# Residual add and RMS norm over 65,536 rows: each tile's store is queued behind five minimum-reductions on VectorE

## Chip, cores, metric

One core of a Trainium2 chip. The metric is device microseconds of one execution. The kernel before takes 3724.74 us (median of 4 runs, 3724.70 to 3724.87). All runs quoted are fast, with a granted clock of 1.0.

## The reference

```python
batch, seq, dim = 32, 2048, 2048          # x, residual: float32; gamma: ones(dim)
z = x + residual
rms = np.sqrt(np.mean(z ** 2, axis=-1, keepdims=True) + eps)
return (z / rms * gamma).astype(np.float32)
```

That is 537 MB of x and 537 MB of residual to read and 537 MB of output to write.

## The kernel before

The rows are cut into tiles of 128 partitions x 7 rows x 2048 columns, 7168 KB each (the first two are smaller, the last is handled in four pieces): 74 tiles, numbered 0 to 73. There are two buffers `z` for x, worked on in place and stored from, and one area `r_area` of 11 rows for the residual. SyncE issues the loads of x and the stores, on one queue; ScalarE issues the residual's loads, on another. VectorE adds, ScalarE takes sums of squares and root, VectorE scales.

```python
z = [sb(f"z{p}", [P, R, D]) for p in range(2)]      # R = 7, D = 2048
r_area = sb("r_area", [P, R + STEP, D])             # STEP = 4
... # cut
def sp_turn(sp, t):                                  # SyncE, tile i - 1 goes out
    i = t.i
    t.wait(sp, "done", -1)
    inc(sp.dma_start(out=rows(o_f, i - 1), in_=z[(i - 1) % 2][:, : sizes[i - 1], :]), "s_out", i - 1)
    ... # cut
    t.wait(sp, "s_out", -1)                          # the store has landed
    load_x(sp, t, 1)                                 # x of tile i + 1, same buffer, same queue
... # cut
def dve_turn(v, t, own):                             # VectorE
    i, p = t.i, t.p
    t.wait(v, "x_in")
    t.wait(v, "r_in")
    (a0, b0), (a1, b1) = parts(i)                    # 3 or 4 of the 7 rows
    inc(add(v, i, a0, b0), "add_a", i)               # lets ScalarE load the next residual
    inc(add(v, i, a1, b1), "add_b", i)
    for h, (a, b) in enumerate(parts(i)):
        n = b - a
        t.wait(v, "rms_a" if h == 0 else "rms_b")
        v.reciprocal(out=rstd[p][h][:, :n], in_=rms[p][h][:, :n]).then_inc(dve, U)
        v.wait_ge(dve, own(i, h))
        ins = scale(v, i, a, b, rstd[p][h])
    inc(ins, "done", i)
```

Of the kernel before, what the change touches and what calls it, by code (L numbers as in the profile page):

```python
# [9 lines left out]
def kernel(  # L10
# [5 lines left out]
    eps: float,  # L16
    out: bass.AP,
):



# [7 lines left out]
    P = nc.NUM_PARTITIONS  # L29
# [20 lines left out]
    last = n_tiles - 1  # L50

    LO = 3
# [12 lines left out]
    def sb(name, shape):  # L65
        return ctx.enter_context(nc.sbuf_tensor(name, shape, fp32))
# [6 lines left out]
    def sem(name):  # L73
        sems.append(ctx.enter_context(nc.semaphore(name)))
        return sems[-1]
# [6 lines left out]
    ssq = [[sb(f"ssq{p}{h}", [P, 4]) for h in range(2)] for p in range(2)]  # L82
    rms = [[sb(f"rms{p}{h}", [P, 4]) for h in range(2)] for p in range(2)]
    rstd = [[sb(f"rstd{p}{h}", [P, 4]) for h in range(2)] for p in range(2)]
    tail_ssq = sb("tail_ssq", [P, R])
    tail_rms = sb("tail_rms", [P, R])
    tail_rstd = sb("tail_rstd", [P, R])
# [8 lines left out]
    dve = sem("dve_own")  # L96
    act = sem("act_own")
    s_tail = sem("s_tail")
    tail_ev = {k: sem(f"tail_{k}") for k in ("add", "rms", "done")}


# [7 lines left out]
    def parts(i):  # L109
        if i == 0:  # L110
            return [(0, 2), (2, sizes[0])]
        k = sizes[i] if i < 2 else R
        return [(STEP, k), (0, STEP)] if i % 2 else [(0, R - STEP), (R - STEP, R)]
# [15 lines left out]
    def inc(ins, kind, i):  # L129
        return ins.then_inc(ev[kind][i % 2], U)  # L130
# [38 lines left out]
    def add(v, i, a, b):  # L169
        e = entry(i)  # L170
        s = z[i % 2][:, a:b, :]
        return v.tensor_add(out=s, in0=s, in1=r_area[:, e + a : e + b, :])  # L172

    def scale(v, i, a, b, rs, c=0):
        for g in range(a, b):
            s = z[i % 2][:, g, :]
            ins = v.scalar_tensor_tensor(  # L177
                out=s,
                in0=s,
                scalar=rs[:, c + g - a : c + g - a + 1],  # L180
                in1=gamma_tile[:, :],
                op0=mult,
                op1=mult,
            )
        return ins

    def dve_turn(v, t, own):
# [3 lines that stand above are left out]
        (a0, b0), (a1, b1) = parts(i)  # L191
        inc(add(v, i, a0, b0), "add_a", i)
# [4 lines that stand above are left out]
            v.reciprocal(out=rstd[p][h][:, :n], in_=rms[p][h][:, :n]).then_inc(dve, U)  # L197
            v.wait_ge(dve, own(i, h))
            ins = scale(v, i, a, b, rstd[p][h])
        inc(ins, "done", i)  # L200


    class Chain:
# [69 lines left out]
    def vector_program(v):  # L273
        v.memset(eps_tile[:, :], float(eps))  # L274
        v.memset(stage, 0.0).then_inc(tail_ev["add"], 1)  # L275
        v.wait_ge(g_in, 4 * U)
        v.stream_shuffle(gamma_tile[:, :].rearrange("p (a b) -> p a b", a=16), stage, [0] * 32)  # L277
        for i in range(LO):
            dve_turn(v, Turn(i), lambda i, h: (2 * i + h + 1) * U)
        with v.Fori(0, 2 * n_iter, 2) as it:  # L280
            for i in range(LO, LO + 2):
                dve_turn(v, Turn(i, it), lambda i, h: it * (2 * U) + (2 * i + h + 1) * U)
        for i in range(HI, last):
            dve_turn(v, Turn(i), lambda i, h: (2 * i + h + 1) * U)
        base = 2 * last * U
        t = Turn(last)
        t.wait(v, "r_in")

        def tail_scale(k):
            a, b = tail[k]  # L290
            v.wait_ge(tail_ev["rms"], k + 1)
            v.reciprocal(out=tail_rstd[:, a:b], in_=tail_rms[:, a:b]).then_inc(dve, U)  # L292
            v.wait_ge(dve, base + (k + 1) * U)
            scale(v, last, a, b, tail_rstd, a).then_inc(tail_ev["done"], 1)

        for k, (a, b) in enumerate(tail):
            v.wait_ge(x_tail[k], U)
            add(v, last, a, b).then_inc(tail_ev["add"], 1)
            if k:
                tail_scale(k - 1)  # L300
        tail_scale(len(tail) - 1)
# [21 lines left out]

    sync_program(nc.sync)
    vector_program(nc.vector)
    scalar_program(nc.scalar)

# [40 lines left out]
```

## Time and profile before

| | before |
|---|---|
| time | 3724.74 us |
| span in the profile | 3723.7 us |
| VectorE, ScalarE, GpSimd busy | 62%, 29%, 0% |
| DMA row | 9 in all 40 slices |

The DMA row gives how busy the 16 DMA engines are. Of the kernel before, with 40 slices of 93 us each:

```profile
GB/s 421 431 434 435 434 434 435 434 435 435 434 434 434 434 434 434 434 434 433 434 434 434 434 434 434 434 434 434 434 434 434 434 434 434 434 434 434 434 432 398
```

What SyncE waits for, in the kernel before (who waited for what: us in total, times, longest):

```profile
SPq L135 <- DMA out_dram<-z: 2828.4, 71, 43.0
SPq L153 <- DVE z L177: 735.1, 73, 32.2
```

About 10 us in each tile it waits for VectorE's done, and about 40 us for the landing of the store that this releases. The second wait is four times the first; the prediction is about what it is made of.

### The profile page before, as it was taken

The numbers are of one execution on the slowest core, as the hardware profiler recorded it, in microseconds if no ns is written. First come the engines' busy times: TensorE is split into PE (matmuls) and PEld (weight loads), VectorE is DVE, ScalarE is ACT, GpSimd is POOL, SyncE is SP. The second block draws the span as 40 slices with busy tenths as digits, with TensorE's granted clock in tenths as the row PEclk, the third lists the DMA queues.
The fourth block names the chain that finished last, engine by engine and source line by source line (L and its number), as shares of the span: only waits on it lengthen the run. The fifth ranks groups of instructions, "written<-read, shape, count | busy, mean of one in ns | idle before, by whom it ended". The sixth has DMA issues, their size and how long they took to land.

```text
span 3723.7 us, 3798 instructions
## 1 busy us (share of the span) xinstructions
DVE 2302.6 (62%) x816; ACT 1072.4 (29%) x1176; POOL 0.2 (0%) x4
## 2 busy tenths in 40 slices
DVE  5666665566665566665566665566665566665566
ACT  2233322233322233322233322233322233322233
POOL 0000000000000000000000000000000000000000
DMA  9999999999999999999999999999999999999999
GB/s 421 431 434 435 434 434 435 434 435 435 434 434 434 434 434 434 434 434 433 434 434 434 434 434 434 434 434 434 434 434 434 434 434 434 434 434 434 434 432 398
DMA packets 32963, 1610.68 MB, mean 433 GB/s; under 512 B 3712, under 2 KB 3776, under 8 KB 3776
## 3 DMA queue, kind: packets, MB, share of 16 engines
q1 hardware_dynamic: 22592, 1082.17, 67.2%
q10 hardware_dynamic: 10368, 528.49, 32.8%
q14 instruction: 3, 0.02, 0.0%
HBM read 1073.77 MB, written 536.87 MB: 433 GB/s over the span
## 4 chain that ended last, share of the span: by engine, by line
DMA 67%; DVE 22%; issue 9%; ACT 2%; SPq 0%; DVEq 0%; ACTq 0%
DMA out_dram<-z 39%; DMA z<-in_x_dram 27%; DVE z L172 15%; DVE z L177 7%; ACT sq_junk L223 1%; ACT rms L231 0%; DVE rstd L197 0%; SPq L259 0%; DVEq L127 0%; DVE r_area L275 0%; ACTq L211 0%; ACTq L127 0%; SPq L141 0%; DVE tail_rstd L292 0%; SPq L162 0%
## 5 line engine op out<-in xcount | busy, mean ns | idle before, releaser
L172 DVE TENSOR_TENSOR z<-z,r_area 128x8192 f32<-128x8192 f32 (+2 forms) x150 | 1109.5, 7437 | 1252.5 <-DMA z<-in_x_dram 1252.5
L223 ACT ACTIVATE sq_junk<-z 128x2048 f32<-128x2048 f32 x512 | 963.4, 1882 | 2617.1 <-DVE z L172 2605.7
L177 DVE SCALAR_TENSOR_TENSOR z<-z,rstd,gamma_tile 128x2048 f32<-128x2048 f32 x505 | 1153.6, 2344 | 5.2
L197 DVE RECIPROCAL rstd<-rms 128x4 f32<-128x4 f32 (+2 forms) x146 | 25.3, 173 | 130.8 <-ACT rms L231 130.8
L223 ACT ACTIVATION_READ_ACCUMULATOR sq_junk<-z 128x1 f32 x512 | 95.5, 186 | 0.0
L231 ACT ACTIVATE rms<-ssq,eps_tile 128x4 f32<-128x4 f32 (+2 forms) x146 | 43.3, 297 | 13.4
L177 DVE SCALAR_TENSOR_TENSOR z<-z,tail_rstd,gamma_tile 128x2048 f32<-128x2048 f32 x7 | 16.2, 2345 | 0.1
L277 DVE LOAD_MASK_SELECT gamma_tile<-r_area x1 | 0.0, 14 | 16.1 <-DMA r_area<-in_gamma_dram 16.1
L277 DVE STREAM_SHUFFLE gamma_tile<-r_area 128x2048 f32<-128x2048 f32 x1 | 2.3, 2290 | 0.0
L275 DVE MEMSET r_area<- 128x2048 f32 x1 | 1.8, 1765 | 0.4 <-issue 0.4
L223 ACT ACT_TABLE_LOAD x1 | 1.3, 1283 | 0.9 <-SPq L77 0.9
L231 ACT ACT_TABLE_LOAD x1 | 1.3, 1283 | 0.1
L231 ACT ACTIVATE tail_rms<-tail_ssq,eps_tile 128x2 f32<-128x2 f32 (+1 forms) x4 | 1.2, 295 | 0.1
L274 DVE MEMSET eps_tile<- 128x1 f32 x1 | 0.1, 59 | 1.0 <-SPq L77 1.0
L292 DVE RECIPROCAL tail_rstd<-tail_rms 128x2 f32<-128x2 f32 (+1 forms) x4 | 0.6, 158 | 0.0
L349 POOL MEMSET const-bfloat16-1.0<- 128x1 bf16 x1 | 0.1, 101 | 0.0
L349 POOL MEMSET const-uint8-127<- 128x1 uint8 x1 | 0.1, 101 | 0.0
L349 POOL MEMSET const-float32-0.0<- 128x1 f32 x1 | 0.1, 98 | 0.2 <-issue 0.2
L349 POOL MEMSET const-float32-1.0<- 128x1 f32 x1 | 0.1, 98 | 0.0
## 6 DMA issues: line engine op xcount, KB each, us to landing
r_area<-in_residual_dram ACTq DMA_DIRECT2D x72, 7168.0 KB, 35.5
z<-in_x_dram SPq DMA_DIRECT2D x71, 7168.0 KB, 27.5
out_dram<-z SPq DMA_DIRECT2D x71, 7168.0 KB, 40.8
z<-in_x_dram SPq DMA_DIRECT2D x3, 2048.0 KB, 17.9
out_dram<-z SPq DMA_DIRECT2D x3, 2048.0 KB, 15.0
r_area<-in_residual_dram SPq DMA_DIRECT2D x1, 5120.0 KB, 25.0
z<-in_x_dram SPq DMA_DIRECT2D x1, 5120.0 KB, 36.7
out_dram<-z SPq DMA_DIRECT2D x1, 5120.0 KB, 26.5
```

The lines of the kernel that those rows point to most:

```text
L172: return v.tensor_add(out=s, in0=s, in1=r_area[:, e + a : e + b, :])
L177: ins = v.scalar_tensor_tensor(out=s, in0=s, scalar=rs[:, c + g - a : c + g - a + 1], in1=gamma_tile[:, :], op0=mult, op1=mult,)
L197: v.reciprocal(out=rstd[p][h][:, :n], in_=rms[p][h][:, :n]).then_inc(dve, U)
L223: s.activation(out=sq_junk[:, :], in_=src[:, g, :], func=Act.Square, accum_out=sq[:, g - a : g - a + 1],)
L231: return s.activation(out=rm, in_=sq[:, : b - a], func=Act.Sqrt, bias=eps_tile[:, :], scale=inv_d)
L274: v.memset(eps_tile[:, :], float(eps))
L275: v.memset(stage, 0.0).then_inc(tail_ev["add"], 1)
L277: v.stream_shuffle(gamma_tile[:, :].rearrange("p (a b) -> p a b", a=16), stage, [0] * 32)
L292: v.reciprocal(out=tail_rstd[:, a:b], in_=tail_rms[:, a:b]).then_inc(dve, U)
L349: nc = _bacc.Bacc("TRN2", target_bir_lowering=False, num_devices=1)
```

## The change

It adds work that nobody needs, ahead of the done signal: from tile 3 on VectorE takes the minimum of a row of 1536 zeros five times in one instruction, waits for it, writes one column and only then calls the tile done. It puts a number on what it costs when a finished tile is handed over late.

```diff
+    zeros = sb("zeros", [P, 1536])
+    least = sb("least", [P, 5])
+    spare = sem("spare")
...
-        inc(ins, "done", i)
+        if i < LO:                                   # LO = 3
+            inc(ins, "done", i)
+        else:
+            v.wait_ge(spare, i - LO + 1 if t.it is None else t.it + (i - LO + 1))
+            v.tensor_reduce(
+                out=least[:, :],
+                in_=zeros[:, :].unsqueeze(1).to_broadcast([P, 5, 1536]),
+                op=mybir.AluOpType.min,
+                axis=mybir.AxisListType.X,
+            ).then_inc(spare, 1)
+            v.wait_ge(spare, i - LO + 2 if t.it is None else t.it + (i - LO + 2))
+            inc(v.memset(least[:, 4:5], 0.0), "done", i)
...
+        v.memset(zeros[:, :], 0.0).then_inc(spare, 1)   # once, at the start
+        v.wait_ge(spare, last - LO + 1)                 # once, before the last tile
```

## The prediction

> **What bounds the kernel now.** I read the page from the top: the engines' shares, the slices, the queues, then the chain of waits, and after that the waits of VectorE and of the DMA queue, and the timeline of one tile.
>
> ```profile
> DVE 2302.6 (62%) x816; ACT 1072.4 (29%) x1176; POOL 0.2 (0%) x4
> DMA  9999999999999999999999999999999999999999
> q1 hardware_dynamic: 22592, 1082.17, 67.2%
> q10 hardware_dynamic: 10368, 528.49, 32.8%
> HBM read 1073.77 MB, written 536.87 MB: 433 GB/s over the span
> DMA 67%; DVE 22%; issue 9%; ACT 2%; SPq 0%; DVEq 0%; ACTq 0%
> DMA out_dram<-z 39%; DMA z<-in_x_dram 27%; DVE z L172 15%; DVE z L177 7%; ACT sq_junk L223 1%; ACT rms L231 0%; DVE rstd L197 0%; SPq L259 0%; DVEq L127 0%; DVE r_area L275 0%; ACTq L211 0%; ACTq L127 0%; SPq L141 0%; DVE tail_rstd L292 0%; SPq L162 0%
> ```
>
> No compute engine is near full, and the DMA row is at 9 in every slice. The chain tells something else at first sight: 22% of it is VectorE work, as if slower vector work would cost directly. It holds that because a buffer's round is store, then load of x into the same buffer, then add, sum of squares, scale, then store. A chain shows what released what, but not that a transfer spent part of its time queued behind another one. For that I take one tile from the timeline:
>
> ```profile
> 1807.81 15.16 DVE L172 TENSOR_TENSOR z<-z,r_area 128x6144 f32<-128x6144 f32 x2 [17.64 <-DMA z<-in_x_dram]
> ...
> 1814.55 0.34 ACTq L141 DMA_DIRECT2D r_area<-in_residual_dram  x1
> ...
> 1831.02 0.33 SPq L135 DMA_DIRECT2D z<-in_x_dram  x1
> ...
> 1831.88 9.12 DVE L177 SCALAR_TENSOR_TENSOR z<-z,rstd,gamma_tile 128x2048 f32<-128x2048 f32 x4
> 1841.03 0.34 SPq L153 DMA_DIRECT2D out_dram<-z  x1
> 1858.63 15.16 DVE L172 TENSOR_TENSOR z<-z,r_area 128x6144 f32<-128x6144 f32 x2 [17.63 <-DMA z<-in_x_dram]
> ```
>
> One tile takes 1858.63 - 1807.81 = 50.82 us. It moves three transfers of 7168 KB, 22.02 MB, which is 433 GB/s. So the tile's time is the transfers' time, and each transfer alone would be 50.82 / 3 = 16.9 us. The landings on the page are longer, because they overlap and queue:
>
> ```profile
> z<-in_x_dram SPq DMA_DIRECT2D x71, 7168.0 KB, 27.5
> out_dram<-z SPq DMA_DIRECT2D x71, 7168.0 KB, 40.8
> ```
>
> The next load of x is issued at 1831.02 and lands at 1858.5. The store is issued at 1841.03, 10.0 us later, on the same queue (SyncE issues both), and lands 40.8 us later, at 1881.83. From the landing of x to there are 23.3 us, which is enough for 16.9 us of store with a residual load beside it from 1865.4 on. So the store moved nothing for its first 17 us: it stood behind the load of x. I checked that x is not shared with it: residual (from 1814.55, landed 1850.05) and x split the engines evenly from 1831 to 1850, so x has done about 9.5 of its 16.9 us, the other 7.4 alone give 1857.5, and 1858.5 is measured. Nothing is left for the store.
>
> **The packet records** of the trace sharpen this. An x or store is 8 packets of 57,344 B on each of 16 DMA engines, 2.12 us each, and 24 packets x 2.12 us = 50.9 us: every DMA engine is busy all the time, not just on average. In each tile in mid-kernel the 16 engines write their semaphore for x between 23.3 and 27.0 us after x was issued (12 of them before 24.3); late in the kernel, around 3400 us, between 21.4 and 27.0. Behind that write an engine takes the store's packets at once. A transfer put on an empty queue gives its first packet 3.4 to 3.9 us after its issue (x, in the tiles I looked at). The store therefore must be issued some 3.5 us before an engine is done with x. It is issued at 10.0, needed at 21.4 - 3.5 = 17.9 for the quickest engine late in the kernel and at 27.0 - 3.5 = 23.5 for the last.
>
> [...]
>
> **The change, part by part.** Removed: nothing. Moved: the done signal of tiles 3 to 72 (70 tiles), from the last scale to a one-column memset behind the reduction.
> - The reduction reads 5 x 1536 = 7680 elements. From the rows
>
> ```profile
> L172 DVE TENSOR_TENSOR z<-z,r_area 128x8192 f32<-128x8192 f32 x72 | 625.3, 8685 | 0.0
> L172 DVE TENSOR_TENSOR z<-z,r_area 128x6144 f32<-128x6144 f32 x71 | 465.6, 6558 | 1242.4 <-DMA z<-in_x_dram 1242.4
> L274 DVE MEMSET eps_tile<- 128x1 f32 x1 | 0.1, 59 | 1.0 <-SPq L77 1.0
> ```
>
> one element more costs (8685 - 6558) / 2048 = 1.039 ns, so 7680 cost 6558 + 1536 x 1.039 = 8.15 us.
> - The memset: 0.06 us. The wait for the reduction's semaphore and the register work: about 0.04 us, as the 0.03 to 0.04 us gaps between reciprocal and scale are. Overlap with the scale before it: -0.06. Sum: 8.2 us later for each store.
> - The zeros' memset at the start, some 1.4 us (1765 ns for 2048 columns), lies in the 16.07 us for which VectorE waits for gamma: nothing.
> - VectorE's busy time: 2302.6 + 70 x 8.21 + 1.4 = 2879 us, 77%. It still waits for x: 17.63 - 8.2 = 9.4 us a tile.
> - SyncE: it waits about 10 us for done and then 40.8 us for the landing of the store. Both ends are fixed by the transfers, so I expect 18.2 and 32.6. The order of transfers on each queue doesn't change, and the residual load, which starts behind the first add of a tile, isn't touched.
>
> In steady state the store is issued at 10.0 + 8.2 = 18.2 us after x and its packets are there at 21.7 to 22.1. In mid-kernel that is before the first engine needs them (23.3). Late in the kernel the quick engines (21.4) would stand still for 0.3 to 0.7 us. They are 3 to 5 us ahead of the last one, and the landing waits for all 16, so this eats of their lead and not of the tile's time; once the lead is a little smaller, they don't stand still any more. Cost: 0.
>
> At the start: store 3 goes from 117.62 to 125.8, its packets are there at 129.4 or so, and x of tile 4 (issued 98.63) leaves the engines at 129.0 to 130.5. At most 0.4 us, once.
>
> At the end: the last done comes at 3679.0 in place of 3670.8, and the tail's first add, at 3676.41 before, starts 2.6 us later. 0.4 us of that are caught up in the idle time before the second add, and the tail's four stores are 2.2 us later. They stand behind the 7168 KB store and are mostly hidden too; the very last, issued at 3708.8 before, now at 3711.0 and ready at about 3714.5, is needed near 3715. I allow 1 us. Sum: 3724.7 + 0.4 + 1.0 = 3726.
>
> **The rivals.**
> 1. The chain counts: a buffer's round is two tiles (101.6 us), and 8.2 us in it would be 70 / 2 x 8.2 = 287 us, 4012 us; this is what the 22% of VectorE in the chain suggest. Against it: the store's first 17 us are queueing.
> 2. [...] At half the rate it takes 16 us, the store is issued at 26 us and ready at 29.6, 2.6 us after the last engine is through x: 70 x 2.6 = 182 us at most, 3907 us. For it speaks only that no reduction is in the trace. Free room is 23.5 - 10.0 = 13.5 us, so the reduction may be 60% slower than I think before this begins.
> 3. The quick engines' standing still is not absorbed: 0.3 to 0.7 us over 70 tiles, 21 to 49 us, up to 3774 us. Against it: the landing of x and of the store is set by the last engine, which has 5 us of room.
> 4. VectorE becomes the bound: 31 us of work a tile plus 8.2 is 39, against 50.8. No.
>
> A gain I see no room for: the bytes and the engines' packets stay.
>
> **Range and chances.** [...] The runs of before lie within 0.2 us. Below, a lucky phase of the engines might give 2 or 3 us; above, the start, the tail and a part of rival 3 some 12. Predicted 3726 us, 3721 to 3738 for 8 in 10. Slower by over 2% (3799) needs rival 1 or 2: 4%. Faster: 1%.
>
> **What would show it.** Right: the reduction at 8.1 to 8.3 us; the store's median landing 32.6 in place of 40.8 and x's still 27.5; VectorE's idle time before an add near 9.4 us; 433 GB/s. The chain may even hold a larger share of VectorE without a longer span. Wrong: x's landing or the tile's 50.8 us grow, or the DMA row shows an 8; a reduction above 13 us would make it so, or stores that need far more than 3.9 us from issue to first packet.

Three passages are cut from it, where marked: a paragraph, the first sentence of rival 2 (the "it" that takes 16 us is the reduction) and a sentence on the range. What is weaker is the reduction's time. No trace before the change has a reduction; the 8.15 us are an estimate that takes the add's 1.039 ns per element (from 8685 and 6558 ns) for it. Estimates are also the overlap of 0.06 us (two adds of 8685 and 6558 ns took 15.16 us together, an overlap of 0.08) and the even split of x and residual. "At once" behind an engine's semaphore write for x is measured: within 0.01 us (938 such pairs in the packet records of the kernel before, 400 to 3500 us). The 23.3 us of the first engine are those near 1831 us; near 1069 us it was 24.4, near 2593 us 22.4.

## The result, and the profile after

3724.91 us, the median of 4 runs (3724.73 to 3725.07), against 3724.74. The ratio is 1.0, with a 95% interval of 0.9983 to 1.0018. (Ratios are the mean time of one kernel's fast runs over that of the other's of the same rounds, so not quite the ratio of the medians quoted.)

So VectorE has 570 us more to do and each of 70 stores is issued later, and the time is the same. The page of the changed kernel (line numbers have moved: the adds are L176, the scales L181, the reduction L208):

```profile
DVE 2872.5 (77%) x957; ACT 1072.4 (29%) x1176; POOL 0.2 (0%) x4
HBM read 1073.77 MB, written 536.87 MB: 433 GB/s over the span
DMA 58%; DVE 30%; issue 9%; ACT 2%; DVEq 0%; SPq 0%; ACTq 0%
L208 DVE TENSOR_REDUCE least<-zeros 128x5 f32<-128x7680 f32 x70 | 570.4, 8148 | 0.0
z<-in_x_dram SPq DMA_DIRECT2D x71, 7168.0 KB, 27.5
out_dram<-z SPq DMA_DIRECT2D x71, 7168.0 KB, 32.5
```

The chain of waits is the trap here. VectorE's share of it went from 22% to 30%, and the reduction stands on it with 8% of the span, some 300 us. And yet the span is not longer: what the reduction put on the chain, the store's landing gave back (40.8 to 32.5 us, 8.3 us less). A chain holds the time from the queuing of a transfer to its landing as one piece, with the standing in line inside.

The same place in the timeline of the changed kernel, where the prediction showed the kernel before:

```profile
1830.72 0.33 SPq L139 DMA_DIRECT2D z<-in_x_dram  x1
...
1831.58 9.12 DVE L181 SCALAR_TENSOR_TENSOR z<-z,rstd,gamma_tile 128x2048 f32<-128x2048 f32 x4
1840.62 8.15 DVE L208 TENSOR_REDUCE least<-zeros 128x5 f32<-128x7680 f32 x1
...
1848.99 0.34 SPq L157 DMA_DIRECT2D out_dram<-z  x1
1858.33 15.16 DVE L176 TENSOR_TENSOR z<-z,r_area 128x6144 f32<-128x6144 f32 x2 [9.36 <-DMA z<-in_x_dram]
```

The store is issued 1848.99 - 1830.72 = 18.27 us after the load of x (10.01 before), the next add starts 27.6 us after that load, as before, and VectorE's idle time before the add is 9.36 us in place of 17.63.

And SyncE's waits in the changed kernel:

```profile
SPq L139 <- DMA out_dram<-z: 2268.9, 71, 35.7
SPq L157 <- DVE least L215: 1244.3, 70, 18.0
```

The two together are 3563.5 us before; here they are 3513.2, and 3581.3 with the waits for tiles 0 to 2, which have no reduction and are listed apart (68.1 us). One wait grew by about what the other lost.

### The profile page after: what moved, and what is told of

Read it like the earlier page. It is cut to its first block, busy times and chain, and to the rows that moved or that the text cites. A ratio compares the mean times of both kernels' runs of the same rounds, so it can differ in the third digit from the quotient of the medians.

```text
span 3723.3 us, 4114 instructions
## 1 busy us (share of the span) xinstructions
DVE 2872.5 (77%) x957; ACT 1072.4 (29%) x1176; POOL 0.2 (0%) x4
## 2 busy tenths in 40 slices
DMA packets 32963, 1610.68 MB, mean 433 GB/s; under 512 B 3712, under 2 KB 3776, under 8 KB 3776
## 4 chain that ended last, share of the span: by engine, by line
DMA 58%; DVE 30%; issue 9%; ACT 2%; DVEq 0%; SPq 0%; ACTq 0%
DMA out_dram<-z 31%; DMA z<-in_x_dram 27%; DVE z L176 15%; DVE least L208 8%; DVE z L181 7%; ACT sq_junk L238 2%; DMA r_area<-in_gamma_dram 0%; ACT rms L246 0%; DVE rstd L201 0%; DVEq L131 0%; SPq L274 0%; DVE r_area L290 0%; DVEq L296 0%; DVE least L215 0%; DVEq L214 0%
## 5 line engine op out<-in xcount | busy, mean ns | idle before, releaser
L176 DVE TENSOR_TENSOR z<-z,r_area 128x8192 f32<-128x8192 f32 (+2 forms) x150 | 1109.3, 7437 | 676.4 <-DMA z<-in_x_dram 676.2
L181 DVE SCALAR_TENSOR_TENSOR z<-z,rstd,gamma_tile 128x2048 f32<-128x2048 f32 x505 | 1153.6, 2344 | 5.2
L208 DVE TENSOR_REDUCE least<-zeros 128x5 f32<-128x7680 f32 x70 | 570.4, 8148 | 0.0
L246 ACT ACTIVATE rms<-ssq,eps_tile 128x4 f32<-128x4 f32 (+2 forms) x146 | 43.3, 297 | 13.4
L181 DVE SCALAR_TENSOR_TENSOR z<-z,tail_rstd,gamma_tile 128x2048 f32<-128x2048 f32 x7 | 16.2, 2346 | 0.1
## 6 DMA issues: line engine op xcount, KB each, us to landing
r_area<-in_residual_dram ACTq DMA_DIRECT2D x72, 7168.0 KB, 35.5
z<-in_x_dram SPq DMA_DIRECT2D x71, 7168.0 KB, 27.5
out_dram<-z SPq DMA_DIRECT2D x71, 7168.0 KB, 32.5
```

Source lines behind the costliest of these rows:

```text
L176: return v.tensor_add(out=s, in0=s, in1=r_area[:, e + a : e + b, :])
L181: ins = v.scalar_tensor_tensor(out=s, in0=s, scalar=rs[:, c + g - a : c + g - a + 1], in1=gamma_tile[:, :], op0=mult, op1=mult,)
L208: v.tensor_reduce(out=least[:, :], in_=zeros[:, :].unsqueeze(1).to_broadcast([P, 5, 1536]), op=mybir.AluOpType.min, axis=mybir.AxisListType.X,
L246: return s.activation(out=rm, in_=sq[:, : b - a], func=Act.Sqrt, bias=eps_tile[:, :], scale=inv_d)
```

## The experiments

The question is what makes 8.3 us free, and how many more would be. D below is the time from the end of the last scale to the issue of the store, from their start times in the trace: 0.03 us before, 8.29 in the changed kernel. t is the time from the issue of the load of x to the issue of the store that stands behind it in the queue: 10.01 and 18.2 us.

The theory at the start (queue room) is the prediction's: the store is free to be late as long as its packets are there when the last DMA engine is through the load of x ahead of it. Rival V: the room is VectorE's idle time of 17.6 us. Rival W: the work itself would cost. Rival C: the chain counts. The result alone rules out C for 8.3 us.

### More repeats: eight (e1_rep8) and ten (e2_rep10)

```diff
-    least = sb("least", [P, 5])
+    least = sb("least", [P, 8])                                    # e2: 10
-                in_=zeros[:, :].unsqueeze(1).to_broadcast([P, 5, 1536]),
+                in_=zeros[:, :].unsqueeze(1).to_broadcast([P, 8, 1536]),
-            inc(v.memset(least[:, 4:5], 0.0), "done", i)
+            inc(v.memset(least[:, 7:8], 0.0), "done", i)
```

> Eight repeats in place of five: the reduction should take 8.15 + 3 x 1536 x 1.039 ns = 12.9 us, the store be issued some 23.1 us after the next load of x, and its packets be there at 26.6 us. Theory (queue room): the last DMA engine is through x at 27.0 us, so the delay is still hidden: 3725 to 3730 us, x lands in 27.5 us as before, the engines' finish of x, spread over 21 to 27 us before, draws together to about 26.5 to 27. Rival V (the room is VectorE's idle time of 17.6 us before the next add): 3725 us too, with no drawing together. Rival C (the chain counts 8.2 us per two tiles): 3725 + 35 x 13 = 4180 us.

> Ten repeats: the reduction should take 16.1 us, the store be issued at 26.3 us after the load of x, its packets be there at 29.8. Theory (queue room): every engine stands still for 29.8 - 27.0 = 2.8 us in each of 70 tiles: 3725 + 195 = 3920 us (3870 to 3960), VectorE still waits for x in every tile. Rival V (VectorE's idle time of 17.6 us is the room): 16.2 us fit, 3725 us. Rival C: 3725 + 35 x 16.2 = 4290 us.

Eight repeats: 3731.83 us (3731.49 to 3736.16, ratio 1.0023, 95% interval 1.0006 to 1.004), near the theory's 3725 to 3730 but 1.8 us above it. D is 13.08. By the packet records of the trace the engines finish x, near 3400 us of the run, between 25.4 and 27.1 us after its issue, where the kernel before had 21.4 to 27.0 there: they drew together, less closely than expected. Most of the 7 us are lost in the tiles: two tiles take 101.77 us in place of 101.60, and packets of the residual's load are stretched by 0.13 us per tile and engine. So the loss does not set in sharply.

Ten repeats: 3829.91 us (3827.83 to 3832.19, ratio 1.0283, 1.0266 to 1.03). That is a loss, so rival V falls: VectorE still has idle time before the add. But it is 105 us, and the theory had said 195. The timeline of ten repeats shows why:

```profile
1908.48 15.16 DVE L176 TENSOR_TENSOR z<-z,r_area 128x6144 f32<-128x6144 f32 x2 [4.33 <-DMA z<-in_x_dram]
...
1931.65 0.33 SPq L139 DMA_DIRECT2D z<-in_x_dram  x1
...
1957.95 0.34 SPq L157 DMA_DIRECT2D out_dram<-z  x1
1959.25 15.16 DVE L176 TENSOR_TENSOR z<-z,r_area 128x6144 f32<-128x6144 f32 x2 [1.32 <-DMA z<-in_x_dram]
...
1984.89 0.33 SPq L139 DMA_DIRECT2D z<-in_x_dram  x1
...
2008.72 0.34 SPq L157 DMA_DIRECT2D out_dram<-z  x1
```

t is 1957.95 - 1931.65 = 26.3 us in one tile and 2008.72 - 1984.89 = 23.8 in the next. A stall pushes the next load of x back, but not the done of the tile that VectorE is working on, so the next store is late by less. The theory took t as the same in every tile. What repeats is the round of a buffer, which is two tiles long. With the figures of this run: the store 27.6 us from issue to the next load (the mean; single tiles have 26.7 to 28.5), load of x 27.5, VectorE's turn from add to last scale 33.2, 0.1 for hand-overs; 88.4 us, plus D. The engines need 101.6 us for two tiles. That these terms add up to two tiles is bookkeeping, true of every run (before: 40.8 + 27.5 + 33.2 + 0.1 = 101.6); what the theory claims is that the store's term falls to about 27.6 us and no further. So **the second theory (a buffer's round)** is: two tiles take the longer of 101.6 and 88.4 + D us; D is free up to 13.2 us, and every us above costs 35 us, not 70.

The page of ten repeats also shows how to read the DMA row:

```profile
DMA  9999999999999999999999999999999999999999
GB/s 424 433 420 419 425 422 414 421 418 421 423 422 417 430 419 416 426 417 422 421 419 424 419 420 419 425 427 419 415 418 420 419 431 418 419 422 419 422 422 403
```

The run lost 2.8%, and the busy row doesn't show it; the GB/s do. The packet records tell why. Between 400 and 3500 us, per tile and engine, 0.48 us are idle, all of them 24 to 28 us after the load of x was issued, and another 0.99 us lie in packets that took longer than the usual 2.12 us (0.39 in packets of the store, 0.60 in packets of the residual, 36 to 44 us after it, where the residual sets in beside the store). Together 1.47 us, and 70 x 1.47 = 103 of the 105 us. So only a third of the loss is engines with nothing to do, which is all that the first theory knows.

### The same work behind the signal (e3_rep10_behind_done), the same delay without the work (e4_gpsimd_delay)

```diff
 # e3, against e2: ten repeats
-        if i < LO:
-            inc(ins, "done", i)
-        else:
+        inc(ins, "done", i)
+        if i >= LO:
...
-            inc(v.memset(least[:, 9:10], 0.0), "done", i)
+            v.memset(least[:, 9:10], 0.0)

 # e4: the kernel before, GpSimd between VectorE's done and SyncE
+    def pool_program(g):
+        g.memset(pad[:, :], 0.0).then_inc(pad_s, 1)           # pad: 128 x 1536
+        with g.Fori(0, 2 * n_iter, 2) as it:
+            for i in range(LO, LO + 2):
+                Turn(i, it).wait(g, "done")
+                for m in range(10):
+                    g.wait_ge(pad_s, it * 10 + (10 * (i - LO) + m + 1))
+                    g.memset(pad[:, :], 0.0).then_inc(pad_s, 1)
...
-        t.wait(sp, "done", -1)
+        if i - 1 < LO:
+            t.wait(sp, "done", -1)
+        else:
+            sp.wait_ge(pad_s, 10 * (i - LO) + 1)
```

> The same ten repeats, but behind the done signal: the same VectorE work, the store as early as in the kernel before. Theory (queue room): the store is issued at 10.0 us again, VectorE is through 1.3 us before the next x lands: 3725 us (3723 to 3730). Rival W (it is the work itself, on VectorE or on the memory the transfers use, that costs): the same loss as with ten repeats ahead of done.

> The kernel before, with no work added to VectorE: GpSimd waits for done, writes zeros ten times (128 x 1536) into a tile of its own, and SyncE waits for GpSimd. How long that is I don't know ahead, the issue of the store against the load of x tells it. Theory (queue room): with a store issued at t us after the load of x the time is 3725 us for t up to 23.5, and 3725 + 70 x (t - 23.5) above, so 3920 us for the 26.3 us that ten repeats on VectorE should give. Rival W (VectorE's work costs, not the late store): 3725 us whatever t.

Ten repeats behind done: 3728.44 us (3728.2 to 3728.67, ratio 1.001, 0.9993 to 1.0026). The timeline of this run:

```profile
1840.91 16.15 DVE L207 TENSOR_REDUCE least<-zeros 128x10 f32<-128x15360 f32 x1
1841.02 0.34 SPq L157 DMA_DIRECT2D out_dram<-z  x1
...
1858.62 15.16 DVE L176 TENSOR_TENSOR z<-z,r_area 128x6144 f32<-128x6144 f32 x2 [1.44 <-DMA z<-in_x_dram]
```

VectorE is 92% busy and 1.44 us short of being late, and nothing is lost in the tiles. The 3.7 us are the end of the program: the last reduction runs until 3686.9 us, so the tail's first add starts at 3687.16 in place of 3676.41, its first store is issued at 3700.99 in place of 3690.41, and by the packet records the engines are only half busy from 3699 to 3719 us. The two runs with ten repeats differ in where the signal stands, and in 101 us.

GpSimd's delay: 3768.56 us (3764.97 to 3769.32, ratio 1.0116, 1.0099 to 1.0132), with VectorE's busy time as before (2302.5 us). The timeline of this run:

```profile
1901.45 9.12 DVE L182 SCALAR_TENSOR_TENSOR z<-z,rstd,gamma_tile 128x2048 f32<-128x2048 f32 x4
1901.76 0.33 SPq L137 DMA_DIRECT2D z<-in_x_dram  x1
1910.72 14.30 POOL L337 MEMSET pad<- 128x1536 f32 x10 [36.49 <-DVE z L182]
1925.05 0.34 SPq L158 DMA_DIRECT2D out_dram<-z  x1
1929.76 15.16 DVE L177 TENSOR_TENSOR z<-z,r_area 128x6144 f32<-128x6144 f32 x2 [19.18 <-DMA z<-in_x_dram]
```

Here D = 1925.05 - (1901.45 + 9.12) = 14.5 us and t = 23.3 in this tile, 23.9 as the mean of 400 to 3500 us. So the late store costs without any work on VectorE: rival W falls both ways. In size, the expectation's formula gives 3725 + 70 x (23.9 - 23.5) = 3753 us, 28 of the 44 us lost; the second theory, 35 x (14.47 - 13.2) = 44. The packet records of this run have next to no idle time behind x (0.03 us a tile); 0.61 us a tile lie in stretched packets where the residual sets in. That goes against the mechanism of the first theory at its onset.

### The second theory put to the test: nine (e5_rep9) and twelve repeats (e6_rep12)

The edit is that of e1, with 9 and 12.

> Nine repeats, between the eight that cost 7 us and the ten that cost 105. Second theory (a buffer's round): store at its shortest 27.6 + load of x 27.5 + VectorE's turn 33.25 + 0.1 = 88.45 us plus the delay D, against the 101.65 us in which the engines move two tiles; free up to D = 13.2, then 35 rounds x (D - 13.2). With D = 14.53 + 0.10: 35 x 1.43 = 50, and some 3 for the tail: 3778 us (3768 to 3788). First theory (each tile pays): 70 x 1.1 = 79, 3804 us. Rival V (VectorE's 17.6 us): 3728 us.

> Twelve repeats, D = 19.31 + 0.10 us. Second theory (a buffer's round): 35 x (19.41 - 13.2) = 217 and some 3 for the tail: 3945 us (3930 to 3960); the stall may lie in every second tile, or evenly. First theory (each tile pays): 70 x 6 = 420, 4145 us. Rival V: VectorE's turn of 33.25 + 19.41 = 52.7 us is the period of a tile: 70 x (52.7 - 50.8) = 130, 3858 us.

Nine: 3772.26 us (3767.72 to 3774.21, ratio 1.0125, 1.0111 to 1.0139), inside the range of the second theory and 32 us from the first. Twelve: 3921.0 us (3919.04 to 3922.27, ratio 1.0526, 1.0511 to 1.0541), 24 us under the second theory's 3945 and just outside its range, 224 us from the first and 63 from rival V. The timeline of twelve repeats shows a term that moved:

```profile
1928.33 0.33 SPq L139 DMA_DIRECT2D z<-in_x_dram  x1
...
1953.80 15.16 DVE L176 TENSOR_TENSOR z<-z,r_area 128x6144 f32<-128x6144 f32 x2 [1.64 <-DMA z<-in_x_dram]
...
1979.07 0.33 SPq L139 DMA_DIRECT2D z<-in_x_dram  x1
...
2006.62 6.56 DVE L176 TENSOR_TENSOR z<-z,r_area 128x6144 f32<-128x6144 f32 x1 [0.18 <-DMA z<-in_x_dram]
```

In every second tile x lands in 25.4 us (1953.76 - 1928.33) and not in 27.5, so in 26.5 as the mean of 400 to 3500 us, while the store's way to the next load takes 27.9 in place of 27.6. Together that is 0.7 us less in a round, and 35 x 0.7 = 25 us, about the 24. The terms of the round are thus not quite fixed. Over all runs, with the means from start times between 400 and 3500 us:

| run | D, us | two tiles, us | two tiles less D |
|---|---|---|---|
| before | 0.03 | 101.6 | |
| changed | 8.29 | 101.6 | |
| eight repeats | 13.08 | 101.8 | 88.7 |
| GpSimd | 14.47 | 102.9 | 88.4 |
| nine | 14.69 | 102.9 | 88.2 |
| ten | 16.28 | 104.6 | 88.3 |
| twelve | 19.48 | 107.2 | 87.7 |

### Part of the store queued early (e7, e8, e9, e10)

If what counts is that the engines have something queued, half a store should do.

```diff
 # e7 (ten repeats) and e8 (no reduction)
-        t.wait(sp, "done", -1)
-        inc(sp.dma_start(out=rows(o_f, i - 1), in_=z[...][:, : sizes[i - 1], :]), "s_out", i - 1)
+        for kind, sent, a, b in (("done_a", "s_a", a0, b0), ("done", "s_out", a1, b1)):
+            t.wait(sp, kind, -1)
+            inc(sp.dma_start(out=rows(o_f, j)[:, a:b, :], in_=z[j % 2][:, a:b, :]), sent, j)
...
+        t.wait(sp, "s_a", -1)
         t.wait(sp, "s_out", -1)
...
             ins = scale(v, i, a, b, rstd[p][h])
+            if h == 0:
+                inc(ins, "done_a", i)
 # e9 (ten repeats) and e10 (no reduction): the loads of x and residual in the same two parts as well,
 # each with its own semaphore; VectorE waits for all four
```

> Ten repeats ahead of done, but each tile's store in two: the part scaled first (3 or 4 of 7 rows, 7.3 us or more of transfer) is queued as soon as it is scaled, only the other waits for the reduction. Theory (room is what the engines have queued): behind x they have another 7.3 us to move, so the second part may be issued up to 30.8 us after x; it is issued at 26.3: the 105 us are gone but for the tail, 3725 to 3735 us. Rival X (the store of the last part lands late whatever is queued before it, and the round is as long as before): 3830 us as with one store.

> The kernel before with the store in two and no reduction, the control of the run above: all theories say 3725 us (3720 to 3728), as the engines are never without work; more packets of smaller size might cost some us.

Two stores with ten repeats: 3861.9 us (3858.34 to 3879.2, ratio 1.0377). Two stores alone: 3869.56 us (3865.5 to 3883.52, ratio 1.0395). Both expectations missed: the split alone costs 145 us. The reduction then costs nothing on top, but a stall that was already there could cover it, so e7 tells nothing. In the page of two stores alone the residual and x land sooner than before, and the store of the first part late:

```profile
r_area<-in_residual_dram ACTq DMA_DIRECT2D x72, 7168.0 KB, 29.2
z<-in_x_dram SPq DMA_DIRECT2D x71, 7168.0 KB, 23.2
out_dram<-z SPq DMA_DIRECT2D x72, 4096.0 KB, 48.8
```

The store's packets are 24 and 32 KB now, and the residual's still 56 KB. In the kernel before, a DMA engine with packets of both queues moves one of each in turn: by the packet records, x's packets start 4.23 us apart on an engine as long as there are residual packets of 2.12 us to put in between. If that holds for unequal packets too, which was not shown, the residual gets more than half, is through in 29.2 us in place of 35.5, and leaves nothing beside the wait for the next x. (In the timeline x is issued 1958.62 - 1935.75 = 22.9 us after the residual, so at most the quicker engines can be through by then.) That was my reading, and the two runs after it tested it by making all packets alike. A clause that told it as a fact is cut from the next expectation, where marked.

> The store in two alone cost 145 us, though no reduction was in it: its packets became 24 to 32 KB beside the residual's 56 KB[...]. Here x, residual and store are all in two parts of 3 and 4 rows, so that the turns are even again, with ten repeats ahead of done. Theory (room is what the engines have queued): the first part of the store covers the wait, and the 105 us of ten repeats are gone: within 15 us of its control without a reduction, the two near 3730 to 3750 us. Rival X (what counts is when the last part of the store is issued): about 100 us above its control.

> The control: all three transfers in two parts, no reduction. If uneven turns were what the two stores alone lost to, 3725 to 3745 us (the residual landing in about 35 us again and x in about 27); if it is the number of transfers or the packet size itself, 3870 us or more.

All in two, no reduction: 3740.85 us (3740.74 to 3741.45, ratio 1.0043). All in two, ten repeats: 3746.34 us (3745.08 to 3747.25, ratio 1.0058). The landings of all in two, no reduction:

```profile
z<-in_x_dram SPq DMA_DIRECT2D x72, 4096.0 KB, 28.1
r_area<-in_residual_dram ACTq DMA_DIRECT2D x72, 4096.0 KB, 32.9
out_dram<-z SPq DMA_DIRECT2D x72, 4096.0 KB, 40.1
```

So both halves of the reading hold in time: with packets alike, 16 us of the 145 us are left, and ten repeats cost 5.5 us above their control and not 105. Per tile the two runs differ by 0.02 us (51.06 and 51.04), 1.2 us in all; most of the rest is the tail, whose first add starts 11.8 us later (in e3 the tail alone cost 3.7 us). The last part of the store is issued as late as ever (SyncE waits 26.1 us a tile for it, 24.4 with ten repeats and one store); rival X falls. What is not shown is the inside of the 145 us. The packet records of e8 have 2.1 us a tile lost: 0.87 in the first 4 us after the issue of x, about two thirds in stretched packets and one third idle, as the reading has it; but 1.23 in the last packets of x, 16 to 20 us after it, just ahead of the store's smaller ones, for which I have no reason.

No version beats both kernels: 1610.68 MB at the 434 GB/s of most slices are 3711 us of the 3725, and no slice of any run has more than 438 GB/s.

## Why the prediction was right, point by point

The time is right (3726 predicted, 3724.91 measured), and so is the main step: a store first stands behind the load of x, so 8.2 us more are free.

- **"Moved nothing for its first 17 us"** holds for the slowest DMA engine only. By the packet records of the tile shown, the store issued at 1841.03 has its first packet at 1854.39, 13.4 us later, 14 of the 16 engines have begun it by 1856.21, and the last begins 17.0 us after the issue. The prediction's own paragraph on packets implies this; for a delay of 8.2 us it makes no difference.
- **The even split of x and residual** from 1831 to 1850 is not there either. By the same records the first packet of x comes at 1834.71, and 12 of the 16 engines are through the residual by 1842.52 (the last at 1849.60), so by 1850.05 x has done 88 of its 128 packets (69%) and not 9.5 / 16.9 = 56% of them. That the check gave 1857.5, near the 1858.5 measured, is luck.
- **The reduction**: 8.15 us predicted, 8148 ns measured. Eight, nine, ten and twelve repeats took 12.95, 14.55, 16.15 and 19.35 us, which is 1.041 ns per element more, where 1.039 was predicted. The store 8.2 us later: 8.26 us.
- **VectorE**: 2879 us predicted, 2872.5 measured; its idle time before an add 9.4 us, 9.36 in the tile shown; landings 32.6 and 27.5 us, 32.5 and 27.5.
- **The quick engines** draw in as predicted, and it costs nothing: by the packet records the first of the 16 was through x 20.8 us after its issue around 3559 us of the kernel before, and 21.5 at the same place of the changed one.
- **The start** was worked out for the wrong tile. The store at 117.62 us is that of tile 2, which has no reduction. The first delayed store is tile 3's, at 164.09 before and 171.98 after, and it cost nothing. The 0.4 us were not there.
- **The end**: the tail's stores are 2.1 us later (first issue 3692.55, before 3690.41) and hidden. The 1 us allowed is more than the 0.17 us between the medians.
- **The 3.5 us from issue to first packet** was a wrong term. It is right for the load of x, which is put on an empty queue while the engines have residual packets (3.65 to 3.75 us in ten tiles near 1850 and 3380 us of the kernel before). For a store that meets engines with nothing to do, twelve repeats show 0.84 us to the first engine and 0.99 to the sixteenth (28 stores, packet records). By the prediction's own sum the room would then have been 27.0 - 0.9 - 10.0 = 16 us. That 13.5 us came out near the 13.2 us worked out from the runs is luck: two errors met, this term and a stall that begins elsewhere. The time predicted for five repeats doesn't rest on it.
- **Rival 2's size** was too high. It said that a reduction of 16 us would cost 70 x 2.6 = 182 us at most; ten repeats (16.15 us) cost 105. The term that was mis-sized is the 70: a stall is paid once in a buffer's round of two tiles, 35 times.
- **Rival 1**, the chain, was wrong as put, but its 35 rounds are the count that fits above the free 13.2 us: the round is the bound as soon as it is longer than two tiles of transfers.
- **A sign of being wrong** that it named, an 8 in the DMA row, would not have come: ten repeats lost 2.8% with a 9 in every slice. The tile's time and the GB/s show it.

**Open**: why the mean of the store's way from issue to the next load stays near 27.5 us from t = 23.9 on. In ten repeats it is 27.6 both in the tiles with t near 23.5 and in those near 26; in twelve it is 26.9 and 28.9 in turn. By the packet records the loss starts in stretched packets of residual and store, in runs where the engines are nearly in step, and not as idle time behind x. Whether being in step causes it, no run here tells.

## What to carry to other kernels

Before pricing a delay off the chain of waits, ask what else stands in the queue ahead of the transfer: a transfer on the chain may have slack inside its own landing time, as here, where the store was issued 10.0 us behind a load of x that landed after 27.5, and 8.3 us more cost nothing. Then write down the round of a buffer (store, load, compute) beside the time the engines need for the same tiles; here the delay was free up to about the difference and cost once per round above it. How short the store's part of the round gets was not predicted: a run had to show it. Judge a DMA-bound kernel by its GB/s, as the busy row stayed at 9 in a run that was 2.8% slower.
